# New figures for a kernel's own scheduler: a port shared by VectorE and GpSimd, other DMA delays, and listed search rounds with moved ranks

## The chip, the core and the metric

The kernel runs on one core of a Trainium2 chip. Five engines of the core work side by side, each through its own list of instructions in a fixed order: TensorE (PE in the profile, its weight loads PEld) multiplies matrices, VectorE (DVE) and ScalarE (ACT) work on elements and can read the accumulator banks, GpSimd (POOL) works on elements in the core's memory, and SyncE (SP) issues the DMA transfers. An instruction that has to wait for a result of another engine holds up everything behind it in its own list.

The metric is the device time in microseconds (us), the median of several executions. A profile records one execution; its span is the time from its first instruction to its last.

## The reference

One layer of a decoder with two kinds of heads, on 4096 tokens of width 1024, in float32. A normalised input goes through one wide projection (3728 columns). Four heads of gated linear attention (GLA) and eight heads of a delta-rule recurrence (RWKV-7) work on its parts, a gate multiplies each result, one output projection brings both together, and a residual addition and a last normalisation follow.

```python
u = rmsnorm(x, norm_w) @ w_in                     # q, k, v, gates of both head groups
o = gla(q, k, v, log_a); o = o * rsqrt(mean(o*o)) * gla_norm_w * silu(gg)
S = S*w + sa*(kk*a) + v*k;  y = S @ r             # per token and head, sa = -S @ kk
y = (groupnorm(y) * ln_w + ln_b + bonus) * silu(rg)
x = rmsnorm(x + concat(o, y) @ w_out, final_norm_w)
```

## The kernel before

The tokens are worked on in 8 blocks of 512. A float32 projection is done as three float16 products (high times high, high times low, low times high), each of 8 matmuls of 128x512; this makes up most of TensorE's work. The 29 column groups of the input weights and the 8 of the output weights are loaded raw once, scaled and split into a high and a low float16 half, and stored to DRAM (`wdr`); later blocks load the halves again. The raw weights land in `x16_1`, the four buffers that afterwards hold the second block's normalised operands (the profile calls both `x16` buffers `x`). Of each weight ScalarE takes the largest magnitude (`amW`, through a TensorE transpose and a VectorE reduction), VectorE makes the scale (`scl`), ScalarE writes the high half and VectorE the low half. The first 13 weights are split right into working buffers (`wr`, `wg`); the later ones go through two buffers `wo`, so that the pass over one for the largest magnitude has to wait until the store of the weight before it has landed.

A block has four RWKV units (pairs of heads). A unit projects its keys and receptances, builds the matrices `W` and `bk` on VectorE, inverts triangular 32x32 blocks by 31 steps of multiply and add on GpSimd (`tm`, `Tc`; in the last unit on VectorE), and then runs a serial chain over 8 chunks of 64 tokens: a matmul, copies by ScalarE into `us`, a matmul, copies, a matmul, and an update on VectorE. The float16 projections of other streams are what TensorE does while this chain waits for its copies. The sums of squares for the normalisation of the second and later blocks are additions of 128x512 on GpSimd.

Buffers are renamed by the kernel when their shape fits, so one name in the profile (`mgr`, `gep`, `f`, `bk`) stands for different data at different times.

The order of all instructions is made by a scheduler in the kernel itself, while the kernel is built. The streams of the program are first run once to record every instruction as a `Step` with an engine, a duration `d` and a delay `lag` until its result can be used. Then `forward` plays all steps through a model of the engines: whenever an engine is free, it takes the ready step with the lowest rank. `backward` plays them from the end, which gives each step a latest time; those times are the ranks of the next `forward`. This is repeated in rounds, `settle` gives tiles new buffers between rounds, and the order with the earliest modelled end is kept and written out. So the durations, delays and ranks in this model decide the order, and nothing else does. Durations come from `cost`; the `call` in `Engine` sets the delays of DMA transfers; class `Array` models TensorE. All instructions of the program are issued at one source line (L483 in the profile before, L533 after the change), so rows of the profile are told apart by their tiles.

Of the kernel before, what the change touches and what calls it, by code (L numbers as in the profile page):

```python
# [45 lines left out]
NP_ = 24  # L46
# [37 lines left out]
def hymba_kernel(ctx, tc, xT, wt, wg, wo, wua, gup, pk, ck, out):  # L84
# [54 lines left out]
    class Array:  # L139


        def __init__(self):
            self.tile, self.form, self.f32, self.one, self.free, self.clock = {}, None, False, 0.0, 0.0, [0, 0.0, True]

        def put(self, t, d, cols, tiles):
            r, c, f32 = tiles
            form = (r[1] - r[0], c[1] - c[0])
            q = [(i, j) for i in range(r[0], r[1]) for j in range(c[0], c[1])]
            turn = form != self.form
            t = max([t, self.free] + [self.tile.get(k, 0.0) for k in (self.tile if turn else q)]) + 0.09 * turn  # L150
# [5 lines left out]
            full = len(q) == 16  # L156
            if full and f32 == 2:
                load = 0.107 * (c[1] - c[0]) / 4
                d = max(0.0, load - self.one) + max(d / 2, load) + d / 2
            for k in q:  # L160
                self.tile[k] = t + (d if full or not f32 or form in ((2, 2), (1, 1)) else 0.66 * d)
            self.form, self.f32, self.one = form, f32 > 0, d / max(f32, 1)
            self.free = t + (d if full or turn and f32 else d / 2 if f32 and form not in ((4, 1), (2, 2), (1, 1)) else 0.014)
# [30 lines left out]
    lease, leases, born, kinds, kind_of = {}, [], [], {}, {}  # L194

    def whole(ap):
        if ap.tensor.name == out.tensor.name:
            return []
        if ap.space == DRAM:
            return [(ap.tensor.name, 0)]  # L200
# [25 lines left out]
    class Step:  # L226


        def __init__(self, n, t0, eng, d, lag, cols, tiles, tab, f):
            self.n, self.t0, self.eng, self.d, self.lag, self.f = n, t0, eng, d, lag, f  # L230
            self.cols, self.tiles, self.tab, self.on, self.to, self.next = cols, tiles, tab, {}, [], None
            self.form = tiles and (tiles[0][1] - tiles[0][0], tiles[1][1] - tiles[1][0])
# [6 lines left out]
    def put(t0, eng, d, lag, cols, tiles, tab, outs, ins, f):  # L239
# [7 lines left out]
        s = Step(len(steps), t0, eng, d, lag, cols, tiles, tab, f)  # L247
# [28 lines left out]
    def forward(rank, ahead=0.0):  # L276


        wait, can, free = {e: [] for e in "VSGTD"}, {e: [] for e in "VSGTD"}, dict.fromkeys("VSGTDH", 0.0)
        pes, tab, run = Array(), 0, None  # L280
        left, ready, start = [len(s.on) for s in steps], [0.0] * len(steps), [0.0] * len(steps)
        end = [0.0] * len(steps)
        for s in steps:
            if not s.on:
                heapq.heappush(wait[s.eng], (0.0, s.n))

        def soonest(e):
            t = pes.free if e == "T" else free["H" if e == "D" else e]
            return t if can[e] else max(t, wait[e][0][0]) if wait[e] else 1e18

        for _ in steps:
            e = min("VSGTD", key=soonest)
            t = soonest(e)
            if t == 1e18:
                return None, None
            while wait[e] and wait[e][0][0] <= t:
                n = heapq.heappop(wait[e])[1]
                heapq.heappush(can[e], (rank[n], n))
            if e == "T":
                x = next((x for x in can[e] if run and x[1] == run.n), None)  # L300
                x = x or min(heapq.nsmallest(12, can[e]), key=lambda x: x[0] - 2.0 * (steps[x[1]].form == pes.form))
                run = steps[x[1]].next
                can[e].remove(x)
                heapq.heapify(can[e])
            else:
                x = heapq.heappop(can[e])
# [29 lines left out]
    def backward(end):  # L336
# [3 lines left out]
        for s in steps:  # L340
            if not s.to:
                heapq.heappush(wait[s.eng], (0.0, s.n))
# [1315 lines left out]
```

## Time and profile before

| what | value |
|---|---|
| median of 3 runs | 2241.07 us (2240.61 to 2241.08) |
| the profiled execution | 2236.66 us, its span 2234.9 us |
| TensorE busy | 2164.9 us (97%), 20190 matmuls |
| VectorE, ScalarE, GpSimd busy | 1676.8, 1318.2, 891.5 us |
| DMA | 325.05 MB, mean 145 GB/s |
| mean granted TensorE clock | 0.991 |

A row of the timeline has the start in us, the duration in us, the engine, the line, the operation, the tile written and those read, the shape, how many equal instructions follow each other, and in brackets how long the engine was idle before and what ended that. A row of the stretches has the stretch, its length, the busy time of each engine, the granted TensorE clock (1.00 is full speed), the DMA share and GB/s. A row of the waits has who waited for whom, the total in us, how often, and the longest.

### The profile page before, as it was taken

What the parts mean: (1) busy time and instruction counts of PE and PEld (TensorE: products, weight loads), DVE (VectorE), ACT (ScalarE), POOL (GpSimd) and SP (SyncE); (2) the same over time, 40 slices, a digit from 0 to 9 for tenths busy, and PEclk for the clock granted to TensorE, in tenths of its full rate; (3) what the DMA queues carried; (4) which work ended last, traced back from release to release, by engine and by line L of the source; (5) the groups of instructions that cost most, each with busy time, mean ns of one, the idle gap of its engine ahead of it and who ended that gap; (6) DMA issues with size and microseconds to landing.
All of it is one profiled execution on the core that took longest, in us unless ns stands there. A gap on an engine that the chain in (4) does not pass through costs nothing.

```text
span 2234.9 us, 53934 instructions
## 1 busy us (share of the span) xinstructions
PE 2164.9 (97%) x20190; PEld 1330.5 (60%) x20190; DVE 1676.8 (75%) x3679; ACT 1318.2 (59%) x3678; POOL 891.5 (40%) x2209
## 2 busy tenths in 40 slices
PE   6999999999999999999999999999999999999987
PEld 3556575556655667566565566656575566655654
DVE  7778879659786777758677677946968658776776
ACT  7677686555655666355575557635665565644552
POOL 3322635553255440733435613360435645044300
PEclk9999999999999999999999999999999999999999
DMA  7577555545445453545434454543444545444432
GB/s 266 176 240 236 144 170 169 159 115 159 137 125 163 146 163 103 154 122 156 150 106 138 130 164 126 153 135 98 143 145 129 151 117 173 112 121 121 117 106 79
DMA packets 274219, 325.05 MB, mean 145 GB/s; under 512 B 129652, under 2 KB 131876, under 8 KB 273956
## 3 DMA queue, kind: packets, MB, share of 16 engines
q1 hardware_dynamic: 273956, 321.60, 48.3%
q8 instruction: 158, 2.59, 0.5%
q14 instruction: 105, 0.86, 0.1%
HBM read 276.45 MB, written 45.05 MB: 144 GB/s over the span
## 4 chain that ended last, share of the span: by engine, by line
PE 79%; DVE 9%; DMA 5%; ACT 4%; issue 2%; POOL 1%; SPq 1%; DVEq 0%; POOLq 0%; ACTq 0%
PE bank L483 68%; PE ch L483 11%; DMA wdr<-wo 1%; DVE bk L483 1%; DVE mgr L483 1%; DVE mgg L483 1%; DVE x L483 1%; DMA wg<-wdr 1%; SPq L483 1%; DMA wr<-wdr 0%; DVE W L483 0%; ACT wo L483 0%; ACT L483 0%; POOL Tc L483 0%; DVE wo L483 0%
## 5 line engine op out<-in xcount | busy, mean ns | idle before, releaser
L483 PE MATMUL bank<-x,wr 128*128 128x512 f16 x2160 | 547.6, 382 | 8.2 <-DMA wr<-wdr 3.2
L483 PE MATMUL bank<-x,wg 128*128 128x512 f16 x1920 | 484.8, 380 | 2.6 <-DVE mgr L483 1.7
L483 PEld LDWEIGHTS <-wr 128*128 128x128 f16 x2640 | 256.6, 100 | 251.9 <-issue 13.8
L483 POOL TENSOR_TENSOR Tc<-Tc,tm 128x60 f32<-128x60 f32 (+24 forms) x961 | 365.0, 380 | 73.3
L483 PEld LDWEIGHTS <-wg 128*128 128x128 f16 x2160 | 210.0, 100 | 209.3 <-ACT wg L483 11.1
L483 PE MATMUL bank<-x,wo 128*128 128x512 f16 x1188 | 285.2, 379 | 0.0
L483 POOL TENSOR_TENSOR tm<-Tc,sv 128x60 f32<-128x60 f32 (+24 forms) x310 | 126.0, 406 | 354.4 <-DMA sv<-nd 191.6
L483 PEld LDWEIGHTS <-wo 128*128 128x128 f16 x1488 | 144.9, 100 | 142.5 <-issue 3.9
L483 POOL TENSOR_TENSOR tm<-Tc,bk 128x60 f32<-128x60 f32 (+24 forms) x372 | 135.3, 364 | 199.1 <-ACT carry L483 37.6
L483 PEld LDWEIGHTS <-x 128*128 128x128 f16 x3096 | 186.7, 99 | 18.0 <-issue 4.2
L483 DVE COPY_PREDICATED W<-mc,bank 64x512 f32<-64x512 uint8 x228 | 162.0, 726 | 14.3 <-PE bank L483 10.6
L483 ACT COPY us<-bank 64x64 f32<-64x64 f32 x496 | 101.9, 206 | 115.9 <-PE bank L483 110.3
L483 PE MATMUL ch<-x,wr 128*128 128x512 f16 x480 | 123.3, 380 | 4.1 <-ACT wr L483 3.2
L483 PE MATMUL bank<-wr,x 128*128 128x128 f16 x1696 | 118.7, 220 | 0.0
L483 POOL TENSOR_TENSOR tm<-Tc,f 128x60 f32<-128x60 f32 (+24 forms) x155 | 62.2, 401 | 121.3 <-DMA f<-nd 51.0
L483 PEld LDWEIGHTS bank<-us,W 128*128 128x128 f32 x496 | 88.4, 190 | 35.4 <-ACT us L483 4.7
L483 POOL MEMSET Tc<- 32x8 f32 (+1 forms) x160 | 23.6, 148 | 213.3 <-DMA td<-Tc 146.4
L483 ACT ACTIVATE psd<-r,PC 128x64 f32<-128x64 f32 x256 | 88.7, 347 | 6.1
L483 PE MATMUL bank<-us,W 128*128 128x64 f32 x496 | 86.9, 257 | 3.0 <-ACT us L483 1.9
L483 ACT ACTIVATE sa<-bank,mu_s 128x512 f32<-128x512 f32 x90 | 61.8, 686 | 45.3 <-PE bank L483 42.1
L483 DVE SCALAR_TENSOR_TENSOR bk<-bank,PC,psd 64x64 f32<-64x64 f32 x140 | 39.6, 283 | 57.9 <-PE bank L483 54.8
L483 PE MATMUL bank<-wg,x 128*128 128x128 f16 x1088 | 79.9, 220 | 0.0
(2300 smaller groups left out, 4493.1 us busy)
## 6 DMA issues: line engine op xcount, KB each, us to landing
wr<-wdr SPq DMA_DIRECT2D x250, 256.0 KB
wg<-wdr SPq DMA_DIRECT2D x188, 256.0 KB
wo<-wdr SPq DMA_DIRECT2D x128, 256.0 KB
x<-in_wt_dram SPq DMA_DIRECT2D x29, 512.0 KB
wdr<-wo SPq DMA_DIRECT2D x24, 512.0 KB
mgr<-in_xT_dram SPq DMA_DIRECT2D x29, 256.0 KB
bk<-nd SPq DMA_DIRECT2D x48, 128.0 KB
mgg<-in_xT_dram SPq DMA_DIRECT2D x23, 256.0 KB
```

The costliest lines, as they stand in the source:

```text
L483: put(t0, self.name, d, lag, cols, tiles, tab, outs, ins, lambda: f(*[moved(x, ids) for x in a], **{k: moved(x, ids) for k, x in kw.items()}))
```

## The change

The computation stays the same. The scheduler gets other figures and rules, and its search other rounds:

- VectorE and GpSimd share a port in the model: an instruction of GpSimd, or one of VectorE with no accumulator operand (some kinds left out, by `shares`), that begins while such an instruction of the other engine runs is made longer by what that one has left.
- SP is taken to issue a DMA every 0.45 us where it was 0.63 us. A load from DRAM is usable 1.6 us after its data (2.0 us for large ones) where it was 2.0 us, 0.6 us more for a broadcast where it was 0.7 us; a store from the core's memory is complete after 0.6, 1.2 or 1.9 us, by its size, where it was always 0.6 us.
- The result of VectorE is usable after 0.13 us and that of ScalarE and GpSimd after 0.18 us, where both were 0.2 us. The durations of VectorE and GpSimd have new constants.
- Two DMA stores into one DRAM tile do not wait for each other.
- The 24 equal rounds become a list of 24. The first ten have no random part; in the others a random number, from a listed seed and of a listed width, is added to each rank of the first pass. The look-ahead, TensorE's preference for the shape that it has, and the slack in giving buffers also come from the list.
- The loops of `forward`, `backward` and `Array.put` are rewritten to run faster in the build, with the same rules but for those above.

```diff
-NP_ = 24
+ROUNDS = ((0, 0.0, 1.083, 2.0, 5.0), (0, 0.0, 0.7, 2.0, 5.0), (0, 0.0, 0.7, 2.0, 5.0), (0, 0.0, 0.7, 2.0, 5.0),
...
+          (75478, 0.0, 0.419, 0.201, 5.0), (27354, 0.0, 0.7, 2.0, 5.0), (4545, 0.161, 0.387, 2.0, 6.127), (91955, 0.165, 0.7, 0.871, 5.0))
...
-                s.follow(wlast[k], got(wlast[k]) if timed and eng != "T" else None)
+                s.follow(wlast[k], got(wlast[k]) if timed and eng != "T" and not (eng == wlast[k].eng == "D" and k[0] in stores) else None)
...
-    def forward(rank, ahead=0.0):
+    def forward(rank, ahead=0.0, bonus=2.0):
...
-                x = x or min(heapq.nsmallest(12, can[e]), key=lambda x: x[0] - 2.0 * (steps[x[1]].form == pes.form))
+                x = x or min(heapq.nsmallest(12, c), key=lambda x: x[0] - bonus * (steps[x[1]].form == pes.form))
...
             elif e == "D":
-                free["H"], free["D"] = t + 0.63, max(t + 1.28, free["D"]) + d
-                end[s.n] = free["D"]
+                free["D"], port = t + 0.45, max(t + 1.28, port) + d
+                z = port
             else:
                 if s.tab is not None:
                     d, tab = d + 1.2 * (s.tab != tab), s.tab
-                end[s.n] = free[e] = t + d
+                if s.port:
+                    d += max(0.0, ends["G" if e == "V" else "V"] - (0.1 if e == "V" else 0.05) - t)
+                    ends[e] = t + d
+                free[e] = z = t + d
...
-            runs = 0.09 if n == 64 or len(o.shape) > 2 and o.shape[-1] == 64 and n == 512 else 0.0
             if op == "transpose" or op == "tensor_copy" and o.shape[0] == 32:
-                return 0.44
-            return max(0.145, (0.11 if n < 256 else 0.085) + (0.08 if fast else 0.04 * (few > 0)) + n / (1920 if fast else 960) + runs)
+                return 0.2 + n / 960
+            runs = 0.13 if n == 64 and psum else 0.09 if len(o.shape) > 2 and o.shape[-1] == 64 and n == 512 else 0.0
+            return (0.075 if n < 256 else 0.11) + 0.05 * (fast and n > 16) + 0.04 * (few > 0 and n > 16) + n / (1920 if fast else 960) + runs
         if eng == "G":
-            return 0.225 + 0.07 * few + n * (2.13 if len(big) > 1 else 0.95) / 960
+            return 0.155 + 0.07 * few + n * (2.0 if len(big) > 1 else 0.4 if not ins else 0.95) / 960
...
+    def shares(op, aps, n):
+        return not any(a.space == PSUM for a in aps) and op not in ("tensor_reduce", "transpose", "memset") and (n > 1 or op in ("tensor_tensor", "scalar_tensor_tensor"))
...
                         if ins[0].space == DRAM:
-                            lag = 2.0 + 0.7 * (o.space != DRAM and ins[0].ap[0][0] == 0)
+                            lag = (1.6 if b < 5e5 else 2.0) + 0.6 * (o.space != DRAM and ins[0].ap[0][0] == 0)
+                        else:
+                            lag = 0.6 if b < 2e4 else 1.2 if b < 2e5 else 1.9
...
-                        d = cost(self.name, op, ins, n, o) + 0.13 * (e is not None and self.name == "S")
+                        d, lag = cost(self.name, op, ins, n, o) + 0.13 * (e is not None and self.name == "S"), 0.13 if self.name == "V" else 0.18
+                        port = self.name == "G" or self.name == "V" and shares(op, aps, n)
...
-        for _ in range(NP_):
+        for seed, wide, ahead, bonus, slack in ROUNDS:
             for i in range(2):
-                start, end = forward(backward(end), 0.7)
-                if best is None or max(end) < best[0]:
+                rank = backward(end)
+                if i == 0 and wide > 0:
+                    for n in range(len(rank)):
+                        seed = (seed * 1664525 + 1013904223) & 0xFFFFFFFF
+                        rank[n] += (seed / 4294967296.0 - 0.5) * wide
+                start, end = forward(rank, ahead, bonus)
+                if i == 0 or max(end) < best[0]:
                     best = max(end), start, list(home)
```

The number of instructions on the engines that compute does not change: 15123 matmuls, 2330 scalar-tensor instructions on VectorE, 2024 tensor-tensor instructions on GpSimd and 1821 DMAs stand in both programs. All that moves is the order on each engine and the buffers that tiles get. Nearly every row of every engine stands elsewhere than before, so only three places are shown, all in the first 70 us, where the program still has few streams to choose from.

**VectorE, the second pair of attention weights.** `amW` is the largest magnitude of a pair of weights, `scl` their scale, `x_1_..` a raw weight, `wg` and `wr` the halves that are written. Before, from the rows of the first unit's `W` and `bk`:

```order
L483 SCALAR_TENSOR_TENSOR xr_216<-bank_0_179,omu_s_119,sa_218 128x512
L483 TENSOR_TENSOR qi_214<-qi_214,mgg_87 128x512
L483 TENSOR_TENSOR W_0_130<-xr_216,EP_229 128x8x64
L483 TENSOR_TENSOR bk_243<-qi_214,gep_213 64x8x64 x2
L483 TENSOR_REDUCE amW_206<-bank_0_183 128x2
L483 TENSOR_SCALAR pw_202<-amW_206 128x2
L483 TENSOR_SCALAR pw_202<-pw_202 128x2
L483 TENSOR_SCALAR scl_175<-pw_202 128x2
```

With the change:

```order
L533 TENSOR_TENSOR x_0_2_0_78<-mgg_88,x_0_2_0_78 128x512
L533 SCALAR_TENSOR_TENSOR mgr_92<-mgr_92,nwx_178,bank_0_183 128x512
L533 TENSOR_TENSOR x_0_3_0_79<-mgr_90,x_0_3_0_79 128x512
L533 TENSOR_REDUCE amW_206<-ch_295 128x2
L533 TENSOR_SCALAR pw_202<-amW_206 128x2
L533 SCALAR_TENSOR_TENSOR wg_231<-x_1_2_0_82,scl_175,wg_230 128x1024
L533 TENSOR_SCALAR pw_202<-pw_202 128x2
L533 TENSOR_SCALAR scl_175<-pw_202 128x2
L533 SCALAR_TENSOR_TENSOR wr_209<-x_1_3_0_83,scl_175,wg_232 128x1024
```

The reduction and the scale of this pair stood behind the first part of `W` and `bk`; they now stand right behind the normalisation of the first block (`x_0_..`), some 40 rows earlier, ahead of the whole first unit.

**GpSimd, the sums of squares of the second block.** Before, behind the last memsets:

```order
L483 TENSOR_TENSOR x_0_0_0_76<-mgg_85,x_0_0_0_76 128x512
L483 TENSOR_TENSOR x_0_1_0_77<-mgg_87,x_0_1_0_77 128x512
L483 TENSOR_TENSOR x_0_2_0_78<-mgr_89,x_0_2_0_78 128x512
L483 TENSOR_TENSOR x_0_3_0_79<-mgr_92,x_0_3_0_79 128x512
L483 TENSOR_TENSOR rgs_266<-rgs_266,ki_244 128x512
L483 TENSOR_TENSOR rgs_266<-rgs_266,v_264 128x512
L483 TENSOR_TENSOR rgs_266<-rgs_266,rgs_265 128x512
L483 TENSOR_TENSOR rgs_266<-rgs_266,bv_267 128x512
```

With the change:

```order
L533 TENSOR_TENSOR gg_293<-gg_293,kf_196 128x512
L533 TENSOR_TENSOR gg_293<-gg_293,cy_199 128x512
L533 TENSOR_TENSOR gg_293<-gg_293,qi_214 128x512
L533 TENSOR_TENSOR gg_293<-gg_293,xr_216 128x512
L533 TENSOR_TENSOR gg_293<-gg_293,v_263 128x512
L533 TENSOR_TENSOR x_0_0_0_76<-mgg_85,x_0_0_0_76 128x512
L533 TENSOR_TENSOR x_0_1_0_77<-mgg_87,x_0_1_0_77 128x512
L533 TENSOR_TENSOR gg_293<-gg_293,go_283 128x512
```

All seven additions (`rgs`, now `gg`) stood behind the four low halves of the first block's operand; five of them now stand ahead of these, the last two among and behind them.

**TensorE, up to the first unit's product of `W` and `bk`.** Before, near the end of that stretch (`wgs` is a small gate weight, `wg_228` the high half of the second pair's first weight):

```order
L483 MATMUL bank_0_184<-x_0_2_0_78,wgs_174 32x512
L483 LDWEIGHTS wgs_174
L483 MATMUL bank_0_184<-x_0_3_0_79,wgs_174 32x512
L483 LDWEIGHTS wg_228
L483 MATMUL ch_295<-x_0_0_0_76,wg_228 128x512
```

With the change, in its middle (`wg_231` is the low half of a weight of the first pair, `wg_232` now the high half of the second pair's first weight):

```order
L533 LDWEIGHTS wg_231
L533 MATMUL bank_0_179<-x_0_3_0_79,wg_231 128x512
L533 LDWEIGHTS wg_232
L533 MATMUL bank_0_183<-x_0_0_0_76,wg_232 128x512
...
L533 LDWEIGHTS wg_232
L533 MATMUL bank_0_183<-x_0_1_0_77,wg_232 128x512
```

Up to the first matmul that reads `W`, TensorE's list had 79 matmuls of 128x512 that read the first block's operand and weights of 128 columns; it now has 120, the 41 more being the rest of the second pair's two projections.

More of the change, by code (lines that the diff above doesn't have):

```diff
@@ L155, in put @@
             d *= 1 if k[2] else 2
[L156 to L161, printed above, removed]
+            if full:
+                if f32 == 2:
+                    d = max(0.0, 0.107 - self.one) + max(d / 2, 0.107) + d / 2
+                tile.clear()
+                self.rest = self.free = t + d
+            else:
+                four = form in ((2, 2), (1, 1))
+                tile.update(dict.fromkeys(q, t + (d if not f32 or four else 0.66 * d)))
+                self.free = t + (d if turn and f32 else d / 2 if f32 and not four and form != (4, 1) else 0.014)
             self.form, self.f32, self.one = form, f32 > 0, d / max(f32, 1)
-            self.free = t + (d if full or turn and f32 else d / 2 if f32 and form not in ((4, 1), (2, 2), (1, 1)) else 0.014)
             return t, d
@@ L274, in put, with link @@
         steps.append(s)
-    def forward(rank, ahead=0.0):
[L279 to L282, printed above, removed]
+    nexts, befores = [], []
+    def link():
+        known = lambda lat: None if lat is None or lat < 0 else lat
+        nexts[:] = [[(m.n, known(m.on[s])) for m in s.to] for s in steps]
+        befores[:] = [[(m.n, m.d, known(lat)) for m, lat in s.on.items()] for s in steps]
@@ L283, in forward @@
+    def forward(rank, ahead=0.0, bonus=2.0):
+        wait, can, free = {e: [] for e in "VSGTD"}, {e: [] for e in "VSGTD"}, dict.fromkeys("VSGTD", 0.0)
+        pes, tab, run, port, ends = Array(), 0, None, 0.0, {"V": 0.0, "G": 0.0}
+        left, ready, start = [len(x) for x in befores], [0.0] * len(steps), [0.0] * len(steps)
+        end, push, pop = [0.0] * len(steps), heapq.heappush, heapq.heappop
         for s in steps:
             if not s.on:
-                heapq.heappush(wait[s.eng], (0.0, s.n))
@@ L309, in forward @@
                     if soon:
[L310 to L317 removed]
+                        y = min(soon, key=lambda y: rank[y[1]])
+                        push(c, x)
+                        w.remove(y)
@@ L354, in backward @@
             elif e == "D":
[L355 to L361 removed]
+                hold, long = max(0.45, s.d), s.d + 1.28
+            free[e], late[n] = t + hold, t + long
+            for m, d, lat in befores[n]:
+                y = t + long - d if lat is None else t + long + lat
+                if y > ready[m]:
+                    ready[m] = y
+                left[m] -= 1
+                if not left[m]:
+                    push(wait[steps[m].eng], (ready[m], m))
         return [-t for t in late]
```

133 lines of the change are left out of this document (75 added, 58 removed), and 4 rows, old and new, of the table ROUNDS.

## The prediction

> **What bounds the kernel now.** I read the page's busy table and its chain first, then four stretches, then TensorE's waits in each, and last the timeline around the longest ones.
>
> ```profile
> span 2234.9 us, 53934 instructions
> PE 2164.9 (97%) x20190; PEld 1330.5 (60%) x20190; DVE 1676.8 (75%) x3679; ACT 1318.2 (59%) x3678; POOL 891.5 (40%) x2209
> PE 79%; DVE 9%; DMA 5%; ACT 4%; issue 2%; POOL 1%; SPq 1%; DVEq 0%; POOLq 0%; ACTq 0%
> ```
>
> TensorE is busy for all but 70.0 us of the span, and the chain that ends last runs over it for 79%. The order on the engines changes and the work does not, so the most that can be won is those 70.0 us, plus what is lost where TensorE's clock is granted at half. Where these lie:
>
> ```profile
> 0.00:64.00 64.00, 39.09 (x218) 18.39 (x219) 51.22 (x120) 44.84 (x86) 22.06 (x41) 0.92 0.72 241
> 64.00:224.00 160.00, 152.63 (x1459) 99.57 (x1460) 129.85 (x297) 114.61 (x251) 49.99 (x134) 0.98 0.72 225
> 224.00:2128.00 1904.00, 1885.29 (x17793) 1160.20 (x17791) 1422.31 (x3079) 1111.49 (x3189) 819.42 (x2034) 1.00 0.47 138
> 2128.00:2234.90 106.90, 87.94 (x743) 52.29 (x728) 73.47 (x185) 47.30 (x153) 0.00 (x0) 0.93 0.30 94
> ```
>
> TensorE idles 24.9 us in the first 64 us, 7.4 in the next 160, 18.7 in the 1904 of the middle, and 19.0 in the last 107. So 230 us of filling and emptying hold as much idle time as two and a half times the whole middle, where only 1% is left. The longest waits of the four stretches, two rows of each where there are two:
>
> ```profile
> PE ch L483 <- ACT wg L483: 10.6, 1, 10.6
> PE bank L483 <- ACT mgr L483: 4.6, 1, 4.6
> PE bank L483 <- ACT f L483: 3.4, 1, 3.4
> PE bank L483 <- DMA wr<-wdr: 3.2, 1, 3.2
> PE bank L483 <- DVE vt L483: 3.0, 5, 1.0
> PE bank L483 <- DVE Vs L483: 2.6, 1, 2.6
> PE bank L483 <- ACT f L483: 2.5, 2, 2.0
> ```
>
> The 4.6 us is the first load of the input, which no order avoids. The 10.6, the 3.4 and the group at the end are taken up below.
>
> **The wait of 10.6 us, and the port.** TensorE runs out of projections at 49.55 us:
>
> ```profile
> 34.64 3.40 PE L483 MATMUL ch<-x,wr 128*128 128x512 f16 x15
> 48.29 1.26 PE L483 MATMUL bank<-x,wgs 128*32 128x512 f16 x20
> 60.16 3.06 PE L483 MATMUL ch<-x,wg 128*128 128x512 f16 x7 [10.61 <-ACT wg L483]
> 63.15 0.49 PE L483 MATMUL bank<-W,bk 64*128 64x128 f32 x2
> 45.97 1.64 DVE L483 SCALAR_TENSOR_TENSOR lr<-xacc,lrs,lr 64x512 f16<-64x512 f32 x1
> 47.65 1.12 DVE L483 TENSOR_TENSOR lrs<-lrs,usc 128x1 f32<-128x1 f32 x1
> 51.23 1.42 DVE L483 TENSOR_SCALAR qi<-mgr,hka 128x512 f32<-128x512 f32 x1
> 54.44 3.41 DVE L483 TENSOR_TENSOR bk<-qi,gep 64x512 f32<-64x512 f32 x2
> 57.89 0.42 DVE L483 TENSOR_REDUCE amW<-bank 128x2 f32<-128x256 f32 x1
> 47.15 1.60 POOL L483 TENSOR_TENSOR rgs<-rgs,rgs 128x512 f32<-128x512 f32 x1
> ```
>
> It waits for the high half of the second weight pair, which ScalarE can write only after the reduction at 57.89, and that reduction stands on VectorE behind the first unit's `W` and `bk`. These are drawn out: one number per partition (`lrs`) takes 1.12 us and ends at 48.77, just when GpSimd's addition ends (48.75). The same shapes where GpSimd is still:
>
> ```profile
> 37.77 0.69 DVE L483 SCALAR_TENSOR_TENSOR lr<-xacc,lr 64x512 f16<-64x512 f32 x1 [0.61 <-ACT lr L483]
> 48.69 0.41 DVE L483 TENSOR_SCALAR gep<-gep 128x512 f32<-128x512 f32 x1
> 60.97 1.38 DVE L483 TENSOR_TENSOR W<-gbc,EP 64x512 f32<-64x512 f32 x2
> ```
>
> So `lr` lost 0.95 us, `qi` 1.01 and the two `bk` 2.03: 4.0 us of the 10.6, by additions that the old model takes to be free of VectorE. The change removes both causes. The pair's reduction moves ahead of the unit, and five of the seven additions move ahead of the time in which VectorE is the one waited for.
>
> Up to the first matmul that reads `W`, TensorE's list now has 120 large matmuls where it had 79. Fifteen of them take 3.24 us from 34.64 to the next instruction at 37.88, 0.216 each; 41 more cover 8.9 us of the 10.6. Behind them the third pair is late next: its reduction still stands behind `bk`. VectorE needs about 2 us from `bk` to its scale (nine short rows) and ScalarE 1.15 us for the half; the 32 products of `W` and `bk` cover 2 us of that, so I book 1.2 us of new wait. The clock adds to it:
>
> ```profile
> 52.70:63.00 10.30, 2.84 (x7) 0.89 (x7) 10.04 (x16) 4.00 (x6) 3.01 (x2) 0.50 0.13 51
> 158.60:165.40 6.80, 5.94 (x19) 3.71 (x20) 3.76 (x9) 3.87 (x14) 5.55 (x17) 0.50 0.81 300
> 1537.50:1541.00 3.50, 1.99 (x51) 1.58 (x48) 3.47 (x7) 3.07 (x9) 0.00 (x0) 0.99 0.52 153
> 1541.00:1544.40 3.40, 3.40 (x27) 2.95 (x26) 3.33 (x5) 0.00 (x0) 0.00 (x0) 0.50 0.02 4
> ```
>
> At half clock 2.84 us of work lost half of itself, 1.4 us. Sum of the first term: -8.9 + 1.2 - 1.4 = **-9 us**. Its bounds are -12 (the whole wait and its clock) and 0 (rival one).
>
> **The wait of 3.4 us, and the store.**
>
> ```profile
> 153.56 0.42 ACT L483 COPY us<-bank 64x64 f32<-64x64 f32 x2
> 157.79 1.06 ACT L483 ACTIVATE wo<-x 128x1024 f32<-128x1024 f32 x1 [3.81 <-DMA wdr<-wo]
> 159.46 0.80 PE L483 MATMUL bank<-f,bk 128*128 128x128 f32 x2 [3.40 <-ACT f L483]
> ```
>
> ScalarE stands before a pass over a raw weight that may not overwrite `wo` until its store has landed, and the copy `f` of the serial chain stands behind it. Two stores of 512 KB are issued at that time. The old figures put the landing 1.28 + 1.46 + 0.6 = 3.3 us after an issue, the new ones at 4.6. This helps where the store is as late as that. But in the new order of ScalarE a pass over `wo` still stands between a copy `us` and a copy `f`. The half-speed stretch that follows (second row above) cost half of 5.94, 3.0 us. Bounds -6.4 and +3.4 (the same once more); I take **-1.5 us**, a quarter of the gain, since the chain's place for the pass is unchanged.
>
> The Trainium skill speaks against this figure: "DMA: Bandwidth & Descriptors", section "Anatomy of one DMA", has about 2.0 us plus the bytes over 436 GB/s, which is an estimate of 3.2 us for 512 KB, near the old figure. Here ScalarE stood 3.81 us, between the two; by the page this term would be 0 and the sum 1.5 us less.
>
> **The middle.** Its 18.7 us of waits are many: weights loaded again (3.2 us above), results of VectorE on the chain (3.0 in five waits), none over 3.2 us. The last two rows of the clock show that short waits count more than once: after a stretch in which TensorE was busy for 1.99 of 3.50 us, it ran 3.40 us at half. The Trainium skill ("TensorE: Matmul & The Clock Gate", Part 1) ties half speed to an idle window of about 3.4 us; this row shows less than that is enough, and the measurement decides. What the new figures give here has no row. It is bounded by -20 (all waits and 1.7 us of clock) and, from the worst stretch of this trace outside filling and emptying, by +15. What speaks for a gain is that the figures come nearer to the rows: SP is seen to issue in less than 0.63, an addition of 60 columns on GpSimd is 0.38 on the mean with VectorE beside it, and the old model has 0.36 as if alone:
>
> ```profile
> L483 POOL TENSOR_TENSOR Tc<-Tc,tm 128x60 f32<-128x60 f32 (+24 forms) x961 | 365.0, 380 | 73.3
> 16.69 0.43 SPq L483 DMA_DIRECT2D gep<-in_ck_dram x1
> ```
>
> Against it: with all its errors the old model let through only 1%. I take **-3 us**, a sixth.
>
> **The end.** In the last 107 us the same units, the same last projections and the same normalisation follow each other in both orders; the last three chunks of the chain and the closing statistics wait on single results (`Vs`, `f`), and no row is seen to move out of it. I take **0**, with bounds of 5 us each way, a quarter of the 19.0 idle.
>
> TensorE's own work costs nothing more: the same 15123 matmuls, and the shape of the array changes 657 times in both lists. If the interleaving is finer elsewhere, the rows of waits will show it.
>
> **Sum.** -9 - 1.5 - 3 + 0 = -13.5 us. The profiled execution took 2236.66 us, 1.8 us around its span; the median of the runs is 2241.07, 4.4 above it. 2236.66 - 13.5 = 2223.2 in a profiled execution, and **2227.6 as a median, so 2228**.
>
> **Rivals.** *One: the gain of the start is handed back.* The raw weights land in the buffers of the second block's operand, so this block starts when the last of 29 weights is split:
>
> ```profile
> 228.44 1.28 DVE L483 SCALAR_TENSOR_TENSOR wo<-x,scl,wo 128x1024 f16<-128x1024 f32 x1
> 235.04 0.68 DVE L483 TENSOR_TENSOR x<-gg,x 128x512 f16<-128x512 f32 x1
> ```
>
> 6.6 us lie between the last split and the first low half of the second block. In VectorE's list the last split is row 395 before and row 411 now, so it is not earlier. If the stream of weights, not TensorE, sets the second block's start, the first term goes to 0: -4.5, so 2236 to 2237. Against it speaks that TensorE idles only 7.4 us from 64 to 224. Chance 0.17.
>
> *Two: the middle gains too.* The better figures remove half the waits there and their clock, 10.5 us in place of 3: 2220. Chance 0.18.
>
> *Three: slower.* The figures for loads are shorter: a read is taken to be usable 0.4 us earlier and the issue 0.18 us shorter, so the weights that every block loads again (250 + 188 + 128 transfers of 256 KB) are issued later before their use. Two lines are enough to see that loads can be late: the wait of 3.2 us above, and a chain piece where one took over 5 us:
>
> ```profile
> 125.76 5.58 DMA wr<-wdr
> ```
>
> If one in sixteen of the 566 (35) comes 0.6 us late, that is 21 us, and a stretch at half clock for one in five of these waits adds 7 x 1.7 = 12: -13.5 + 33 = +19.5, so 2261. It decides from 13.5 + 4.5 = 18 us of such waits on. For it: the random part of the ranks makes no order more robust against a late transfer. Against it: only 5.6 us of waits on reloaded weights stand in the middle now, and DMA is busy for 0.47 there. Chance 0.13.
>
> *Four: the change does little*, the waits only go to other places and all terms are near 0: 2240. Chance 0.10.
>
> **Numbers.** The forecast has 0.42, rivals 0.17, 0.18, 0.13 and 0.10. This kernel's runs tell 0.2% (4.5 us) from no change. Faster, below 2236.6: the forecast (0.42), two (0.18), and about half of one (0.09): 0.69. Slower, above 2245.5: three: 0.13, and a little of four, together 0.14. The rest, 0.17, is the same. The forecast's own range is 2219 to 2236 (its terms half as large and half as large again, with the end's 5 us). The range that leaves out 2 in 10 reaches up over one and four to 2244 and down below two to 2212.
>
> **What would show it.** Right, if in the profile after, TensorE's wait for `wg` near 50 us is gone or below 4 us; the granted clock of 0 to 64 us is above 0.92; the long VectorE rows there are back to 0.4 to 0.7 us; the first matmuls on `W` still stand near 63 us but with 41 more large ones before; and the middle idles 12 to 19 us. Wrong, if the idle time of 64 to 260 us grows by what the first 64 lose (rival one), or if waits on `wr<-wdr` and `wg<-wdr` in the middle exceed 15 us (rival three).

## The result, and the profile after

The changed kernel takes 2222.08 us (median of 6 runs, 2220.06 to 2228.47) against 2240.84 us before: 0.9928 of the time before, 95% interval 0.9916 to 0.9940. It is faster by 0.7%, about 16 us. 2228 was forecast, with a range of 2212 to 2244. The profiled execution took 2224.65 us. It lies 12.0 us under the profiled execution of before (2236.66), so the profiles hold some 12 of the 16 us; where the rest lies they can't show. The page after:

```profile
span 2222.8 us, 53967 instructions
...
PE 2162.6 (97%) x20190; PEld 1326.6 (60%) x20190; DVE 1669.9 (75%) x3679; ACT 1308.1 (59%) x3678; POOL 865.4 (39%) x2209
...
PE 83%; DVE 8%; DMA 3%; ACT 2%; issue 1%; SPq 1%; DVEq 0%; ACTq 0%
```

TensorE idles 60.2 us, where it was 70.0, and runs over 83% of the chain that ends last, where it was 79%. The four stretches of the forecast, after the change (the last one is 12 us shorter):

```profile
0.00:64.00 64.00, 39.48 (x209) 19.32 (x210) 42.93 (x110) 44.50 (x86) 22.42 (x41) 0.97 0.85 278
64.00:224.00 160.00, 153.10 (x1430) 96.58 (x1429) 133.42 (x300) 106.78 (x234) 58.36 (x134) 0.96 0.69 215
224.00:2128.00 1904.00, 1891.29 (x17905) 1164.80 (x17905) 1428.51 (x3128) 1115.21 (x3225) 784.63 (x2034) 1.00 0.47 138
2128.00:2222.80 94.80, 78.71 (x652) 45.87 (x650) 65.03 (x144) 41.60 (x135) 0.00 (x0) 0.93 0.34 104
```

The first 64 us idle 24.5 us, as before (24.9). The middle idles 12.7 us where it was 18.7. But equal times hold unequal work. So every matmul is given the usual distance to the next one of its kind (the median in the trace before, at full clock), and the stretches are cut where TensorE has done 60, 200 and 1950 us of such work. (A row gives the stretch, its length, and then the busy times of TensorE, its weight loads, VectorE, ScalarE and GpSimd.) Before:

```profile
0.00:100.85 100.85, 74.84 (x531) 41.24 (x532) 78.82 (x177) 69.60 (x130) 33.60 (x73) 0.95 0.73 237
100.85:260.46 159.61, 151.56 (x1461) 97.17 (x1460) 136.91 (x305) 118.45 (x285) 68.59 (x164) 0.98 0.64 203
260.46:2099.17 1838.71, 1821.78 (x17105) 1119.11 (x17102) 1362.53 (x2936) 1073.61 (x3085) 788.55 (x1969) 1.00 0.47 138
2099.17:2234.90 135.73, 116.77 (x1100) 72.94 (x1098) 98.59 (x263) 56.57 (x178) 0.74 (x5) 0.95 0.35 104
```

After the change:

```profile
0.00:100.04 100.04, 74.41 (x556) 42.74 (x556) 74.72 (x176) 68.27 (x127) 29.73 (x59) 0.98 0.74 235
100.04:261.03 160.99, 155.20 (x1340) 94.45 (x1339) 129.77 (x297) 112.16 (x266) 73.00 (x175) 0.96 0.66 208
261.03:2090.07 1829.04, 1817.82 (x17194) 1117.49 (x17191) 1367.10 (x2938) 1066.30 (x3103) 761.94 (x1972) 1.00 0.47 139
2090.07:2222.80 132.73, 115.15 (x1108) 71.88 (x1106) 98.31 (x269) 61.37 (x183) 0.74 (x5) 0.95 0.34 102
```

The four lengths differ by -0.8, +1.4, -9.7 and -3.0 us: 12.1 us, which is the difference of the spans. **Four fifths of the gain lie in the middle, and the start, where the forecast put two thirds, gave nothing.** In the middle 5.7 us are idle time and 4.0 are busy time, of which up to 3.4 are the two half-speed stretches (397.5 to 400.9 and 1541.0 to 1544.4 before) that are gone. How many us fall to which stretch hangs on the price that each kind of matmul gets: with the median distance to the next matmul of any kind, the first two stretches together get 3.8 us longer and the middle 13.3 us shorter. That the middle holds the gain and the start none stays; a middle is known to some 5 us.

### The profile page after: what moved, and what is told of

It reads as the page before. It is cut to its first block, busy times and chain, and to the rows that moved or that the text cites. A ratio compares the mean times of both kernels' runs of the same rounds, so it can differ in the third digit from the quotient of the medians.

```text
span 2222.8 us, 53967 instructions
## 1 busy us (share of the span) xinstructions
PE 2162.6 (97%) x20190; PEld 1326.6 (60%) x20190; DVE 1669.9 (75%) x3679; ACT 1308.1 (59%) x3678; POOL 865.4 (39%) x2209
## 4 chain that ended last, share of the span: by engine, by line
PE 83%; DVE 8%; DMA 3%; ACT 2%; issue 1%; SPq 1%; DVEq 0%; ACTq 0%
PE bank L533 72%; PE ch L533 11%; DVE W L533 1%; SPq L533 1%; DVE x L533 1%; DMA wdr<-wo 1%; DMA wg<-wdr 0%; DVE mgr L533 0%; DVE gt L533 0%; DVE wo L533 0%; DVE vt L533 0%; DMA x<-in_wt_dram 0%; DVE SC L533 0%; ACT wo L533 0%; DVE Ta L533 0%
## 5 line engine op out<-in xcount | busy, mean ns | idle before, releaser
L533 PE MATMUL bank<-x,wr 128*128 128x512 f16 x2392 | 619.5, 381 | 1.8 <-DMA wr<-wdr 1.3
L533 PE MATMUL bank<-x,wg 128*128 128x512 f16 x1736 | 452.7, 381 | 2.8 <-ACT sv L533 1.6
L533 PEld LDWEIGHTS <-wr 128*128 128x128 f16 x2832 | 274.4, 100 | 257.6 <-issue 12.8
L533 PE MATMUL bank<-x,wo 128*128 128x512 f16 x1326 | 320.6, 380 | 0.0
L533 PEld LDWEIGHTS <-wg 128*128 128x128 f16 x1968 | 190.5, 100 | 178.8 <-issue 10.8
L533 PE MATMUL bank<-wg,x 128*128 128x128 f16 x1376 | 108.3, 219 | 0.8 <-DMA wg<-wdr 0.8
L533 PE MATMUL bank<-wr,x 128*128 128x128 f16 x1216 | 96.5, 219 | 0.1
L533 ACT ACTIVATE sa<-bank,mu_s 128x512 f32<-128x512 f32 x91 | 62.4, 686 | 57.1 <-PE bank L533 55.8
L533 ACT ACTIVATE psd<-rk,PC 128x64 f32<-128x64 f32 x256 | 88.7, 346 | 5.7
L533 DVE SCALAR_TENSOR_TENSOR sv<-bank,PC,psd 64x64 f32<-64x64 f32 x154 | 43.5, 282 | 58.4 <-PE bank L533 55.3
L533 ACT COPY sv<-bank 64x64 f32<-64x64 f32 (+2 forms) x216 | 59.4, 275 | 35.4 <-PE bank L533 30.8
```

The costliest lines, as they stand in the source:

```text
L533: put(t0, self.name, d, lag, cols, tiles, tab, port, outs, ins, lambda: f(*[moved(x, ids) for x in a], **{k: moved(x, ids) for k, x in kw. ...
```

## The experiments

Two theories were put against each other. **F**: the figures come nearer to the chip, so that the order that looks best to the model is good on the chip. **S**: the listed rounds with their moved ranks are a lucky draw, whatever the figures. "Port and constants" below are the rule of the shared port together with the new constants of VectorE and GpSimd.

### Each half alone

`e1` has the new figures with the rounds of before:

```diff
-ROUNDS = ((0, 0.0, 1.083, 2.0, 5.0), ...
+ROUNDS = ((0, 0.0, 0.7, 2.0, 5.0),) * 24
-                if i == 0 or max(end) < best[0]:
+                if best is None or max(end) < best[0]:
```

> All new figures and rules, but the 24 equal rounds of before with no random part, and the best order of all rounds kept. Theory F (the better figures carry the gain, the listed rounds are only a draw of a few us): 2220 to 2230, and TensorE's idle time between 224 and 2100 us near the 12.7 us of the change. Theory S (the listed rounds with their moved ranks carry it, the figures nothing): 2235 to 2243, idle time there near the 18.7 us of before.

`e2` has the listed rounds with the figures of before:

```diff
-                        port = self.name == "G" or self.name == "V" and shares(op, aps, n)
+                        port = False
-                free["D"], port = t + 0.45, max(t + 1.28, port) + d
+                free["D"], port = t + 0.63, max(t + 1.28, port) + d
-                            lag = (1.6 if b < 5e5 else 2.0) + 0.6 * ...
+                            lag = 2.0 + 0.7 * ...
-                            lag = 0.6 if b < 2e4 else 1.2 if b < 2e5 else 1.9
+                            lag = 0.6
... (cost as before; results usable after 0.2 us; stores into one DRAM tile wait for each other)
```

> The listed rounds with the old figures, no port rule. Theory F: 2235 to 2245, idle time in the middle near 18.7 us. Theory S: 2218 to 2230, near 12.7 us. If both e1 and e2 stand near 2232, each carries about a half.

The last two lines of the edit of `e1` belong to the rounds: the kernel before keeps the best order of all rounds, the change the best of the last round.

Measured: `e1` 2245.12 us (1.0029, 1.0013 to 1.0045), `e2` 2252.53 us (1.0058, 1.0039 to 1.0077). Both lie above every range that was expected; TensorE idles 15.6 us from 224 to 2100 us in `e1` and 33.8 in `e2`. Each half alone is slower than the kernel before, and both together are faster by 0.7%. Neither theory stands in its simple form, and the gain can't be split into two addends.

### The DMA figures

```diff
-                free["D"], port = t + 0.45, max(t + 1.28, port) + d
+                free["D"], port = t + 0.63, max(t + 1.28, port) + d
-                hold, long = max(0.45, s.d), s.d + 1.28
+                hold, long = max(0.63, s.d), s.d + 1.28
-                            lag = (1.6 if b < 5e5 else 2.0) + 0.6 * ...
+                            lag = 2.0 + 0.7 * ...
-                            lag = 0.6 if b < 2e4 else 1.2 if b < 2e5 else 1.9
+                            lag = 0.6
```

> The change with the four DMA figures of before (0.63 us per issue on SP, reads usable 2.0 us after their data and 0.7 more for a broadcast, stores 0.6 us). If the new DMA figures are what made the first 64 us no better (they take loads to be faster than they are when the queue is full), then TensorE's first projections start before 28 us where they start at 31.5 with the change, and the first 250 us get 3 to 8 us shorter. If the DMA figures carry a gain in the middle, its idle time goes back towards 18.7 us, and the sum is 2225 to 2240. If they do nothing: 2219 to 2227.

`e8` has the same edit, and 20 rounds more at the end of the list (in `e7`, `e8` and `e10` the slack of the round ahead of the new ones is changed too).

> The change with the DMA figures of before, as e3, with a list of 44 rounds found for it in the same way as for e7. If the DMA figures carry nothing and port and constants do, it gains over e3 (2222) what e7 gained over the change: 2212 to 2219. If the DMA figures matter: 2222 to 2230, behind e7 (2216.5).

Measured: `e3` 2221.97 us (0.9922, 0.9895 to 0.9949), `e8` 2217.91 us (0.9907, 0.9888 to 0.9927). With the old DMA figures the gain is all there, so it does not need the new ones. The late start, though, hangs on them: under the list of the change the first projections start at 18.08 us in `e3` and 17.62 in `e8`, with the old DMA figures, and at 31.50 in the change and 29.05 in `e7` (below), with the new ones, as the expectation of `e3` has it. The figures alone don't make it: `e1` and `e12` (below), with the new DMA figures and equal rounds first, start at 21.23 and 21.59. It takes the figures and this list together.

### Port and constants

`e4` leaves out the port rule alone (`port = False`, as in `e2`).

> The change without the rule of the shared port; VectorE's and GpSimd's new constants stay. Theory P (the port rule carries the gain): 2232 to 2242, and the time that instructions of the two engines are drawn out by each other is back at that of before. Rival: the rule is worth nothing by itself, since TensorE is the bound and both engines have slack: 2218 to 2228.

`e10` also has the old constants; four rounds are added to the list:

```diff
+                        port = False
+            runs = 0.09 if n == 64 or len(o.shape) > 2 and o.shape[-1] == 64 and n == 512 else 0.0
             if op == "transpose" or op == "tensor_copy" and o.shape[0] == 32:
-                return 0.2 + n / 960
+                return 0.44
+            return max(0.145, (0.11 if n < 256 else 0.085) + (0.08 if fast else 0.04 * (few > 0)) + n / (1920 if fast else 960) + runs)
...
-            return 0.155 + 0.07 * few + n * (2.0 if len(big) > 1 else 0.4 if not ins else 0.95) / 960
+            return 0.225 + 0.07 * few + n * (2.13 if len(big) > 1 else 0.95) / 960
```

> The change without the port rule and with the constants of before for VectorE and GpSimd (averages in which the drawn-out rows are contained); DMA figures, delays of results and the rule on stores stay new. The list of the change with four more rounds found for these figures, which win 8 us in their own model, as e7's win 8. If the port rule and the constants that go with it carry the gain: 2230 to 2242, no better than e6. If they carry none of it: 2212 to 2222, near e7 (2216.5).

Measured: `e4` 2326.93 us (1.0387, 1.0355 to 1.0420), `e10` 2256.53 us (1.0069, 1.0042 to 1.0096). Both are slower than either side expected. The new constants are those of an undisturbed instruction; without the rule that draws instructions out they are far too short, and the order is 105 us worse than that of the change. With the old constants, which hold the drawn-out rows in their averages, the order is 34 us worse than the change. Each of these is one order. The new delays of results and the new rule on stores are still in `e10`, so they don't carry the gain alone.

### More search

`e7`: new figures, 8 rounds more. `e12`: new figures, 24 equal rounds and 7 more. `e6` and `e11`: old figures (the edit of `e2`), 24 equal rounds and 10 and 9 more. The edit is the list alone, here that of `e12`:

```diff
-ROUNDS = ((0, 0.0, 1.083, 2.0, 5.0), (0, 0.0, 0.7, 2.0, 5.0), ...
+ROUNDS = ((0, 0.0, 0.7, 2.0, 5.0), ..., (19769, 0.088, 0.7, 0.193, 5.0), (26130, 0.0, 0.539, 2.0, 5.0))
```

> The new figures with another, longer list of rounds: 32 of them, found by trying rounds and keeping the one whose order ends earliest in the kernel's own model. If the gain of the change comes from a search under figures that are near enough to the chip, more search gives more: 2208 to 2219. If the orders that the search finds are only draws, whatever the model says of them: anywhere from 2215 to 2250, as e1 and e2 spread.

> The old figures, no port rule, with a list of 34 rounds that was found for these figures in the same way and in the same time as that of e7, and that won as much by their own model (10 us over the kernel before, 8 us over the change in e7). Theory F (search pays only under figures that are near the chip): 2233 to 2245, no better than before. Theory S (the search carries the gain, whatever the figures): 2226 to 2232, some 10 us under before.

> A second list of 33 rounds found for the old figures, from another start of the random choice (7 us won in their own model). It tells how far two searched orders of one set of figures lie apart. If search under the old figures pays nothing, as e6 says: 2233 to 2246. If e6 was an unlucky draw: 2226 to 2233.

> All new figures, 24 equal rounds as in e1 (2245), and 7 more found for these figures, 8 us won in their own model: built up as e6 and e11 are, only with the new figures. If a model near the chip makes search pay whatever its first rounds are (theory F): 2230 to 2238, 7 to 15 us under e1. If the good place of the change and of e7 is that of their first 24 rounds, a lucky draw: 2238 to 2248, no better than e1.

Measured: `e7` 2216.52 us (0.9900, 0.9886 to 0.9915), the fastest of all, and `e12` 2233.80 (0.9966, 0.9951 to 0.9980); `e6` 2236.43 (0.9987, 0.9976 to 0.9998), `e11` 2246.92 (1.0028, 1.0009 to 1.0046). All four lists look 7 to 10 us better than their starting point to their own model. On the chip the two new ones gain 0.28% over the change and 0.63% over `e1`, some 6 and 14 us; the two old ones gain 0.13% and lose 0.28% against the kernel before. That is for theory F: search pays where the model is near the chip. But orders of one set of figures lie far apart (`e1` and `e7` by 29 us), and of the lists that begin with 24 equal rounds `e12` is only 0.2% ahead of `e6`; `e1` may have been a poor order to start from. That the listed rounds were a good path under the new figures is a part of the gain, and how large a part stays open; how the list of the change was found is not on record.

### What stands behind it: SyncE's queue behind GpSimd

One number tells the two sets apart in every profile. SyncE issues all DMAs in one order, and among them those that read `Tc`, the result of GpSimd's steps (`td<-Tc`). How long SyncE stood waiting for GpSimd's `Tc`, from 260 to 2080 us, in the waits of its queue, first before, then with the change, then in `e10`:

```profile
SPq L483 <- POOL Tc L483: 93.6, 27, 14.8
```

```profile
SPq L533 <- POOL Tc L533: 53.8, 22, 7.2
```

```profile
SPq L528 <- POOL Tc L528: 76.3, 31, 8.7
```

Beside it, in the same stretch, the sum of TensorE's waits for weights that are loaded again (`wr`, `wg`, `wo` from `wdr`), and the length of the middle (200 to 1950 us of work). `e9` is the change run once more.

| run | port and constants | DMA figures | ratio to before | middle | SyncE behind `Tc` | waits for reloads |
|---|---|---|---|---|---|---|
| before | old | old | 1 | 1838.7 | 93.6 | 5.6 |
| `e2` | old | old | 1.0058 | 1861.2 | 80.3 | 7.1 |
| `e6` | old | old | 0.9987 | 1834.1 | 82.3 | 6.7 |
| `e11` | old | old | 1.0028 | 1846.3 | 98.0 | 8.6 |
| `e10` | old | new | 1.0069 | 1864.4 | 76.3 | 14.1 |
| `e4` | new, no port | new | 1.0387 | 1911.8 | 144.1 | 23.8 |
| change | new | new | 0.9928 | 1829.0 | 53.8 | 0.9 |
| `e9` | new | new | 0.9937 | 1829.3 | 54.5 | 0.5 |
| `e1` | new | new | 1.0029 | 1837.1 | 57.1 | 1.1 |
| `e7` | new | new | 0.9900 | 1828.7 | 58.4 | 3.6 |
| `e12` | new | new | 0.9966 | 1838.5 | 43.9 | 1.0 |
| `e3` | new | old | 0.9922 | 1824.6 | 38.4 | 1.5 |
| `e8` | new | old | 0.9907 | 1819.8 | 46.6 | 0.5 |

With the port rule and its constants SyncE stands 38 to 58 us behind `Tc` and TensorE waits 0.5 to 3.6 us for reloads; without, 76 to 144 us and 5.6 to 23.8 us. No run falls between. How the one leads to the other is seen at the longest wait for a reload in `e10`, in the timeline of GpSimd, VectorE, SyncE and TensorE:

```profile
238.02 3.22 POOL L528 TENSOR_TENSOR tm<-Tc,bk 128x63 f32<-128x63 f32 x1
240.34 0.74 DVE L528 SCALAR_TENSOR_TENSOR kf<-kf,nwx,go 128x512 f32<-128x512 f32 x1
241.69 3.54 POOL L528 TENSOR_TENSOR tm<-Tc,bk 128x60 f32<-128x60 f32 x1
...
255.35 0.31 POOL L528 TENSOR_TENSOR Tc<-Tc,tm 128x60 f32<-128x60 f32 x1
255.74 1.24 POOL L528 TENSOR_TENSOR tm<-Tc,bk 128x66 f32<-128x66 f32 x1
...
264.23 0.22 POOL L528 TENSOR_TENSOR Tc<-Tc,tm 128x8 f32<-128x8 f32 x1
264.47 2.90 SPq L528 DMA_DIRECT2D td<-Tc  x4
272.77 0.40 SPq L528 DMA_DIRECT2D wg<-wdr  x1
275.47 0.61 PE L528 MATMUL bank<-x,wg 128*128 128x512 f16 x1 [6.66 <-DMA wg<-wdr]
```

Three steps of 60 to 66 columns take 3.22, 3.54 and 1.24 us where one of 60 takes 0.31. VectorE is busy without a gap during the first, with operands in the core's memory, until the row `kf` ends at 241.08; the step ends at 241.24. So the chain of steps ends some 7 us late, SyncE stands 8.7 us at `td<-Tc`, the load of `wg` behind it is issued at 272.77 only, and TensorE waits 6.66 us. The 3.2 us of the forecast's row in the kernel before are the same thing: SyncE stands 4.4 us behind `Tc` until 390.6, and

```profile
392.51 0.42 SPq L483 DMA_DIRECT2D wr<-wdr  x1
397.47 1.89 PE L483 MATMUL bank<-x,wr 128*128 128x512 f16 x4 [3.19 <-DMA wr<-wdr]
```

The new figures do not make GpSimd's steps much shorter. A step `Tc<-Tc,tm` takes 380 ns on the mean before, 368 with the change, and 367 in `e4` and `e10`; the old constants give 337 for the mean step, the new ones 260 for an undisturbed one. The constants of `e4`, without the rule, are furthest off, and SyncE stands longest behind `Tc` there (144.1 us). So what sets the runs apart is whether the model knows when the steps end, not how often they are drawn out. This is argued: the model's own times with the rule are not on record.

The table also shows less than the whole gain. `e1` and `e12` have short waits for reloads and a middle hardly better than before: they wait elsewhere, above all on results of VectorE (11.7 and 7.6 us from 260 to 2080 us, against 6.5 before and 4.8 with the change). And `e6`, with old figures and 82.3 us behind `Tc`, has a shorter middle than both. So the waits for reloads are what the figures change for certain (some 5 us, and up to 1.7 us of half clock behind the one at 397.47); the rest of the middle differs from order to order. Whether the rule alone, with the old constants, would do was not tried.

### The start

In `e5` one transposition of the third weight pair is repeated 16 times, in the order of the change; the result is the same.

```diff
+                steps[-1].whole = self.name == "T" and steps[-1].form == (4, 4) and kw.get("start") is True and kw.get("stop") is True
...
             s.f()
+            if s.whole and start[s.n] > 50 and more:
+                for _ in range(more):
+                    s.f()
+                more = 0
```

> The order of the change, with one transposition of the third weight pair (near 57 us) repeated 16 times on TensorE, 0.29 us each by the four that take 1.16 us in the kernel before: 4.6 us more work there, nothing else moved. If TensorE's own work sets the time from there on, every landmark behind it and the end come 4 to 5 us later (2226 to 2227). If the time up to the second block is set by something beside TensorE (the weights, the first units' chain), the delay is used up in waits that end there anyway: under 1.5 us of it are left from 180 us on, and the end moves by less than 2 us (2221 to 2224). The second would explain why 9 us won at the start need not reach the end.

`e9` is the change, unedited.

> The change itself, once more, for a second profile of the same order. 2220 to 2228 again. Where its landmarks differ from those of the first profile, no cause is read out of the first: up to 3 us at one place (a load that lands late, a stretch at half clock that falls otherwise), and 2 us at the end.

Measured: `e5` 2230.52 us (0.9965, 0.9951 to 0.9979), 8 us over the change; `e9` 2225.26 us (0.9937, 0.9917 to 0.9958). The transpositions took 4.18 us in one row where they took 0.61. Since all three profiles have the same order, one instruction can be followed: transpositions on VectorE near 209 us, the last split of a weight, and a matmul that reads a reloaded `wr`, in the change, in `e9` and in `e5`:

```profile
209.05 1.55 DVE L533 STREAM_TRANSPOSE Ta<-W 32x128 f32<-32x128 f32 x4
240.62 1.29 DVE L533 SCALAR_TENSOR_TENSOR wo<-x,scl,wo 128x1024 f16<-128x1024 f32 x1
789.18 1.25 PE L533 MATMUL bank<-x,wr 128*128 128x512 f16 x5 [0.73 <-DMA wr<-wdr]
```

```profile
206.12 1.55 DVE L533 STREAM_TRANSPOSE Ta<-W 32x128 f32<-32x128 f32 x4
237.85 1.29 DVE L533 SCALAR_TENSOR_TENSOR wo<-x,scl,wo 128x1024 f16<-128x1024 f32 x1
788.23 1.25 PE L533 MATMUL bank<-x,wr 128*128 128x512 f16 x5 [0.53 <-DMA wr<-wdr]
```

```profile
211.87 1.55 DVE L533 STREAM_TRANSPOSE Ta<-W 32x128 f32<-32x128 f32 x4
238.92 1.28 DVE L533 SCALAR_TENSOR_TENSOR wo<-x,scl,wo 128x1024 f16<-128x1024 f32 x1
793.34 2.16 PE L533 MATMUL bank<-x,wr 128*128 128x512 f16 x5 [2.08 <-DMA wr<-wdr]
```

At 209 us `e5` is 2.8 and 5.8 us behind the other two, so the 3.6 us of added work are not used up by then. At 240 us they can't be seen: `e5` lies between the other two. In between the change and `e9` run in part at half clock and `e5` does not: from 200 to 230 us the granted clock is 0.83, 0.89 and 1.00 (rows in the last section), which is up to 5.1 and 3.3 us of lost work. So the stretch does not show that the stream of weights takes up a delay, as the second expectation has it. At 790 us `e5` is 4 to 5 us behind: it waits 2.08 us for the reload, and its five matmuls then take 2.16 us where they took 1.25. At the end it is 5 to 7 us behind. Neither expectation is met. Followed instruction by instruction, TensorE's rows in the change's own two profiles differ by up to 4.2 us (near 210 us), more than the 3 us expected, so no cause can be read out of one such place; the medians (5 to 8 us) say that the end does move, by more than the work added, and why is open.

What happens to a better start is seen in `e3`. The first 64 us and the next 66 of `e3`, and then its longest waits from 64 to 160 us:

```profile
0.00:64.00 64.00, 49.13 (x273) 23.49 (x274) 50.19 (x136) 52.73 (x102) 13.29 (x36) 1.00 0.85 287
64.00:130.00 66.00, 55.31 (x507) 39.80 (x506) 57.37 (x100) 37.54 (x66) 35.62 (x68) 0.87 0.59 177
```

```profile
PE bank L533 <- DVE vt L533: 5.6, 1, 5.6
PE bank L533 <- DVE sv L533: 4.7, 2, 2.4
```

The stretch from 64 to 130 us of the kernel before:

```profile
64.00:130.00 66.00, 64.90 (x590) 41.81 (x591) 53.29 (x112) 45.02 (x82) 24.28 (x63) 1.00 0.70 216
```

`e3` is 10.0 us ahead in TensorE's busy time at 64 us (49.13 against 39.09) and gives 9.6 us of it back by 130 us, with the clock at 0.87. The rows `sv` and `vt` are its waits for VectorE's `bk` (renamed `sv` and `vt`), ahead of the products of `W` and `bk` at 72 and 117 us. Before the first of them VectorE is drawn out beside GpSimd's additions (until 73.23); its row of the same shape behind them is not:

```profile
70.36 1.74 DVE L533 SCALAR_TENSOR_TENSOR sv<-xr,ta 64x512 f32<-64x512 f32 x1
74.26 0.69 DVE L533 SCALAR_TENSOR_TENSOR sv<-xr,ta 64x512 f32<-64x512 f32 x1
```

So the cause of the forecast's first wait is there once more, at another place.

## Why the prediction was right, and where it was wrong

**What bounds the kernel** was read rightly: TensorE's idle time went from 70.0 to 60.2 us and the chain still runs over it. (The three parts that idle 51.3 us beside the middle are 331 us long, 64 + 160 + 107, and not 230; the sum does not use this.)

**The first term (-9 us) failed.** Its row is gone as foretold: no wait for `wg` near 50 us, and the granted clock of the first 64 us is 0.97. But the wait moved to an earlier place. After the change, around 22 us (SyncE, ScalarE, TensorE):

```profile
23.97 0.37 SPq L533 DMA_DIRECT2D x<-in_wt_dram  x1
25.36 1.12 ACT L533 CAST x<-mgg 128x512 f16<-128x512 f32 x2
29.29 1.06 ACT L533 ACTIVATE wo<-x 128x1024 f32<-128x1024 f32 x1 [0.72 <-DMA x<-in_wt_dram]
30.49 1.22 PE L533 MATMUL ch<-ident,amW 128*128 128x128 f32 x4 [8.37 <-ACT wo L533]
31.50 1.91 PE L533 MATMUL bank<-x,wr 128*128 128x512 f16 x4
```

The step that failed is "41 more cover 8.9 us of the 10.6". They do stand ahead of the first `W` now; but with the second pair its transpositions moved ahead of the first projections too, and these wait for a raw weight whose load SyncE issues at 23.97 us. The casts of the first block's operand also come at 25.36, where they came at 16.88 before. So the projections start at 31.50 us and not at 19.92, and the first matmuls on `W` come at 70.31 us, where the forecast left them near 63. The additions of GpSimd that moved ahead now draw out the second pair's own scale (1.12 and 1.20 us at 37.01 and 38.16, for 0.17 us of work). The forecast followed the moved pair on VectorE and TensorE and did not follow it to SyncE and to the load that it now waits for first. After 60 us of work 0.8 us are left, 2.3 in the second profile.

**Rival one** (0.17), that the gain of the start is handed back, could not come into play, since the change won nothing there. `e3`, another order, won it and gave it back by 130 us, at another place: not the start of the second block, but VectorE's `W` and `bk` for the first two units.

**The second term (-1.5 us, the store) came to nothing.** The wait of 3.40 us behind `wdr<-wo` is gone, but from 60 to 200 us of work the change loses 1.4 us, and nothing in the second profile (159.7 us). `e3` and `e8`, with 0.6 us for a store, gain as much as the change. The Trainium skill ("DMA: Bandwidth & Descriptors", "Anatomy of one DMA") made this term 0, by a figure that the section gives for transfers issued from GpSimd; here SyncE issues them. The runs agree with the 0; no run tests the figure. The place itself was not mended either: ScalarE still stands before passes over `wo`, up to 5.59 us (at 214.04), for a store to land.

**The middle (-3 us) had a right cause and the wrong size**: -9.7 us, -9.4 in the second profile. The cause is shown for about half of these (the reloads). The forecast named GpSimd's additions that are drawn out beside VectorE, but not the way from there to TensorE, over SyncE's queue and the reloads; so it took a sixth of the waits where a third of the idle time and all of the half clock went. Its row for GpSimd, 0.38 us, is a mean over 25 shapes and not one of 60 columns; those take 0.43 on the mean, so the old 0.36 was further off than it says. In size this is rival two (10.5 us in the middle, 0.18).

**The end (0)** gave 3.0 us, 2.8 in the second profile, within the 5 us that were allowed.

**Rival three** (0.13) had the sign wrong: the waits for reloads went from 5.6 to 0.9 us, and with the new port and constants the DMA figures neither cause nor cure them (`e3` 1.5, `e8` 0.5). Without them it stays open: `e10`, one order, has 14.1 us with the new DMA figures, and the four with the old ones have 5.6 to 8.6.

The sum was right by luck: the 9 us that failed at the start and the 7 us too few in the middle nearly cancel. It was made for a profiled execution (2223.2, measured 2224.65) with 4.4 us on top for the median; that addition was chance, since the change's own profiled execution lies 2.6 us above its median.

## What to carry to other kernels

An in-order DMA queue ties engines together that have nothing to do with each other: when loads for TensorE stand behind stores of GpSimd's results, an error in the model's durations of GpSimd is paid by TensorE (6.66 us at one place in `e10`), so follow a moved step to the queue that feeds it before booking its gain. Measure the durations in a scheduler's model undisturbed only if the disturbance is modelled too; constants and contention rule belong together (`e4`, 4.6% behind the change). One order is one draw: with these figures two draws differ by up to 1.3%, so a change of a scheduler is judged by several orders of each kind.

## What the runs showed of the hardware that was not expected

The wait for the shared port hits the shortest instructions hardest. VectorE's `scl` (two numbers per partition) and GpSimd's addition, after the change:

```profile
19.91 0.17 DVE L533 TENSOR_SCALAR pw<-pw 128x2 int32<-128x2 int32 x1
20.10 1.26 POOL L533 TENSOR_TENSOR gg<-gg,kf 128x512 f32<-128x512 f32 x1 [12.95 <-ACT gg L533]
20.11 1.27 DVE L533 TENSOR_SCALAR scl<-pw 128x2 int32<-128x2 int32 x1
```

The same kind of instruction takes 0.17 us just before the addition begins, and 1.27 when it begins 0.01 us behind it: it ends with the addition. The Trainium skill ("SBUF — State Buffer", "SBUF: two separate sides") has the port as a lock that one instruction holds for its whole length while the other blocks; these rows agree. A step of GpSimd can also be held for longer than one instruction of VectorE: in `e10` (above) steps of some 0.3 us took 3.22 and 3.54 us beside rows of VectorE that followed each other without a gap, none longer than 1.27 us.

The same order does not lose its half-speed stretches at the same places. From 200 to 230 us the clock granted was 0.83 in the change's first profile, 0.89 in the second and 1.00 in `e5`:

```profile
200.00:230.00 30.00, 26.58 (x206) 16.26 (x205) 23.48 (x64) 15.11 (x38) 0.73 (x5) 0.83 0.62 178
```

```profile
200.00:230.00 30.00, 24.95 (x197) 16.15 (x197) 23.29 (x63) 16.21 (x41) 0.00 (x0) 0.89 0.53 163
```

```profile
200.00:230.00 30.00, 26.19 (x248) 16.77 (x246) 27.26 (x73) 16.76 (x42) 0.73 (x5) 1.00 0.71 212
```

A stretch of 3.4 us at half clock costs up to 1.7 us, so the same order can win or lose 5 us between 200 and 230 us; what decides it is not shown. A single profile is no measure of a few us at one place.
